# Moving the first transfers of a hybrid encoder layer: sample rows in quarters, norm scales from ScalarE's queue, sinks and later parameters under the first SwiGLU

## The chip, the core and the metric

One core of a Trainium2 chip runs the whole program. The metric is device time in microseconds (us) of one execution; three executions of the kernel before are given. The engines are TensorE (PE), VectorE (DVE), ScalarE (ACT), GpSimd (POOL) and SyncE (SP); each works through its own list of instructions in order. In the kernel before every transfer between DRAM and on-chip memory is asked for from SP's list; the moving itself is done by 16 DMA engines.

## What is computed

One layer of a streaming encoder on 512 prompt rows and 8 x 16 sample rows, all fp32, model width 1024:

```
x += 0.5 * SwiGLU_1(rmsnorm(x) * norm_ffn1)
h  = rmsnorm(x) * norm_mix;  P = h @ w_in
A  = sliding-window attention with per-head sinks (attn_sinks)
B  = HGRN2 linear recurrence;  C = conv(4) -> RG-LRU
x += (sig(gA)*A@w_attn_o + sig(gB)*B@w_hgrn_o + sig(gC)*C@w_lru_o) @ w_out
x += 0.5 * SwiGLU_2(rmsnorm(x) * norm_ffn2)
```

Prompt and sample rows share all weights, so the kernel stacks them into 640 columns. Besides x the kernel needs some small parameter vectors: three norm scales, convolution weights, biases, gate parameters, head norms (together 99 rows of 128 numbers) and the 16 attention sinks.

## The kernel before, in words

The activations are kept transposed, 8 chunks of 128 features by 640 columns. Every fp32 product is made of three products of rounded parts: x is split into a high and a low part (RA for the first SwiGLU's input), and so is each weight tile. A weight tile is 1024 x 128 (512 KB). `proj` asks for it into one of three buffers `wr`, makes the high part `wh` (line 654) and the low part `wl` (line 655), and issues for each of the 8 chunks a set of six matmuls of 320 columns (line 659) into one of two psum buffers `pp`.

At the start `load_x` (line 479) brings x. The prompt comes in four quarters of 256 features (`x0`, 512 KB each), the sample rows in one transfer (`xs`, 512 KB). Each quarter is transposed on TensorE into `me` and `ml`, copied out, scaled by `norm_ffn1` and split by `Norm.split` (lines 599 to 602: high part on ScalarE, low part on VectorE). ScalarE also squares the 20 row tiles (line 505) to get the row sums; `first_rstd` (line 507) turns them into RS, the reciprocal root per column, by ten small products on TensorE (lines 518 and 519). The matmuls of the first SwiGLU do not wait for RS; it multiplies their result (`scaled`, line 662).

`load_params` (line 523) asks for parameter rows one vector at a time into the single buffer `pst`, transposes them on TensorE (line 537) and copies them to PRM. It is called once for `norm_ffn1` inside `load_x`, and once for the 91 later rows (line 695 and 696) before the first SwiGLU. PRM's later rows feed `lru_params` (line 551) and, from the end of the first SwiGLU on, everything else. The sinks go to `SK` by ten transfers in `attention` (lines 744 to 748): for each parity of heads one of 64 partitions x 8 numbers and four of 16 x 8, all read with a stride of two numbers.

The order on each engine is not the order of the text. `Sched.run` (line 236) is a planner: it keeps a model of every engine's time, and again and again takes the operation that can start first by that model; among those that start within 0.04 us it takes the one with the lowest priority number (line 161). An operation made later has a higher number; `lag` lowers it by so many projections (`S.item` counts them). A transfer is 0.47 us on SP by the model, and its data take bytes / 250 GB/s behind the earlier ones (line 287). A buffer of a tag with several slots costs 0.15 us at its first use, a fixed buffer like `SK` nothing, so a transfer into `SK` with no predecessor can be planned at time 0. Because of this, one of the ten sink transfers stands first in SP's list and the others wherever the plan leaves SP free. In the hardware program the engines then wait for each other by semaphores, in that fixed order.

`ffn` (line 677) runs three blocks of 8, 8 and 6 features tiles; in each, two up-projections per tile (gate and value) and then eight down-projections.

Of the kernel before, what the change touches and what calls it, by code (L numbers as in the profile page):

```python
# [16 lines left out]
P = 128  # L17
# [73 lines left out]
def ap_of(x):  # L91
    return x() if isinstance(x, View) else x
# [218 lines left out]
def trunk_kernel(ctx: ExitStack, tc: tile.TileContext, A: dict, O: list):  # L311
    nc = tc.nc
    S = Sched()
# [7 lines left out]
    def dve(n, f, aps=0):  # L321
        return ("DVE", 0.066 + 1.042e-3 * n + 0.063 * aps, f)

    def act(n, f, aps=0, src=None):
        return ("ACT", 0.1 + 0.833e-3 * n + 0.093 * aps - (0.049 if src is not None and src.in_psum else 0.0), f)

    def pol(n, f):
        return ("POOL", 0.1 + n * 1e-3, f)

    def pick(alts, only):  # L330
        return [a for a in alts if only is None or a[0] in only]

    def tt(out, a, b, op, only=None):
        alts = [dve(out.n, lambda: nc.vector.tensor_tensor(out(), a(), b(), op=op))]  # L334
        return S.op(pick(alts, only), [a, b], [out])
# [15 lines left out]
    def fn(out, a, func, scale=1.0, bias=0.0, accum=None):  # L351
        aps = isinstance(scale, View) + isinstance(bias, View) + (accum is not None)
        kw = {}

        def f():
            if accum is not None:
                kw["accum_out"] = accum()
            nc.scalar.activation(out(), a(), func, bias=ap_of(bias), scale=ap_of(scale), **kw)  # L358

        return S.op([act(out.n, f, aps, a)], [a, scale, bias], [out] + ([accum] if accum is not None else []),  # L360
                    func=None if func in ANY_TABLE else func)

    def cp(out, a, only=None):
        alts = [act(out.n, lambda: nc.scalar.copy(out(), a()), 0, a),  # L364
                dve(out.n * (1.0 if a.in_psum else 0.5), lambda: nc.vector.tensor_copy(out(), a()))]
        if only is not None and "POOL" in only:
            alts.append(pol(out.n, lambda: nc.gpsimd.tensor_copy(out(), a())))
        return S.op(pick(alts, only), [a], [out])
# [5 lines left out]
        alts = [pol(out.n, lambda: nc.gpsimd.memset(out(), val)), dve(out.n, lambda: nc.vector.memset(out(), val))]  # L374
        return S.op(pick(alts, only), (), [out])

    def dma(out, a, lag=None):
        v = out if isinstance(out, View) else a
        return S.op([("SP", 0.47, lambda: nc.sync.dma_start(ap_of(out), ap_of(a)))], [a], [out],  # L379
                    dma=v.n * 4 * v.proto.shape[0], lag=lag)  # L380

    def mm(calls):

# [14 lines left out]
    def tr(calls):  # L398

        def f():  # L400
            for o, i, d in calls:
                nc.tensor.transpose(o(), i(), d())  # L402

        return S.op([("PE", sum(0.002 + 0.835e-3 * c[0].n for c in calls), f)], [x for c in calls for x in c[1:]], [c[0] for c in calls])


    def fixed(name, shape, dt=F32):
        return Buf(None, sb(name, shape, dt))

    RA = fixed("RA", [P, 16, T], F32R)  # L410
    RB = fixed("RB", [P, 16, T], F32R)
    RS = fixed("RS", [P, T])
    ident = fixed("ident", [P, P])
# [3 lines left out]
    NPRM = 99  # L417
    PRM = fixed("PRM", [P, NPRM])
# [4 lines left out]
    SK = fixed("SK", [P, 32])  # L423
# [45 lines left out]
    xp = A["x_prompt"][0].rearrange("(t p) d -> p t d", p=P)  # L469
    xs = A["x_sample"].rearrange("b t d -> (b t) d")  # L470
# [5 lines left out]
    def xk(m):  # L476
        return X.v.r("p (k t) -> p k t", k=KD)[:, m, :].at(m)

    def load_x():
        bs = S.buf("xs")  # L480
        xin = []
        for c in range(4):
            b = S.buf("x0")
            v = b.v.r("p (t d) -> p t d", t=4)
            dma(v, xp[:, :, c * 256:(c + 1) * 256], lag=(12, 2.5, 1.9, 1.8)[c])
            xin.append(v)
            if c == 0:
                dma(bs.v, xs, lag=12)
                load_params(("norm_ffn1",), 0, 8, lag=12)
        xv = X.v.r("p (k t) -> p k t", k=KD)  # L490
        for c in range(4):
            pb = S.buf("ml")
            for h in range(2):
                pa, o = S.buf("me"), slice(h * P, (h + 1) * P)
                tr([(pa[:, t * P:(t + 1) * P], xin[c][:, t, o], ident.v) for t in range(4)])
                cp(xk(2 * c + h)[:, 0:TP], pa.v, only=("DVE", "ACT"))
            tr([(pb[:, h * P:(h + 1) * P], bs[:, (2 * c + h) * P:(2 * c + h + 1) * P], ident.v) for h in range(2)])
            for h in range(2):
                cp(xk(2 * c + h)[:, TP:T], pb[:, h * P:(h + 1) * P], only=("DVE", "ACT"))
                n1.split(2 * c + h, xk(2 * c + h))  # L500
        for c in range(4):
            tiles = [xin[c][:, t, :] for t in range(4)] + [bs[:, c * 256:(c + 1) * 256]]
            for t in range(NT):
                j = S.buf("sq")
                fn(j[:, 0:256], tiles[t], AF.Square, accum=ss[:, t, c:c + 1].at((t, c)))
# [14 lines left out]
        cp(RS[:, 0:TP], pa.v, only=one)  # L520
        cp(RS[:, TP:T], pb[:, 0:P], only=one)

    def load_params(names, r0, r1, lag=None):
        b = S.buf("pst")
        for name, r, c in (("norm_ffn1", 0, 8), ("norm_mix", 8, 8), ("norm_ffn2", 16, 8), ("conv_b", 24, 8),
                           ("conv_w", 32, 32), ("lru_b_a", 64, 8), ("lru_b_x", 72, 8), ("lru_lambda", 80, 8),
                           ("hgrn_lb_logits", 88, 8), ("hgrn_o_norm", 96, 1)):
            if name in names:
                src = A[name][0].rearrange("j (k p) -> (j k) p", p=P) if name == "conv_w" else A[name].rearrange("o (k p) -> (o k) p", p=P)
                dma(b[r - r0:r - r0 + c, 0:P].at(r), src, lag=lag)  # L530
        for r, name in ((97, "q_norm"), (98, "k_norm")):
            if name in names:
                for h in range(2):
                    dma(b[r - r0:r - r0 + 1, h * 64:h * 64 + 64].at((r, h)), A[name], lag=lag)
        ps = S.buf("ml")
        n = r1 - r0
        tr([(ps[:, :n], b[:n, :P], ident[:n, :n])])
        cp(PRM[:, r0:r1].at(r0), ps[:, :n], only=("DVE",))

    G1, GM, G2, CVB, CVW, BA, BX, LAM, LBL, ON, QN, KN = 0, 8, 16, 24, 32, 64, 72, 80, 88, 96, 97, 98  # L540

# [45 lines left out]
    def hv(v):  # L587
        return v.r("p (a b) -> p a b", a=2)

    def pv(ps):  # L590
        return ps.v.r("p (a b) -> p a b", a=2)[:, :, :HT]
# [70 lines left out]
    def scaled(tag, ps, late=False):  # L662

        b = S.buf(tag)
        if late:
            cp(hv(b.v), pv(ps), only=("ACT", "DVE"))
            tt(b.v, b.v, RS.v, ALU.mult)
        else:
            tt(hv(b.v), pv(ps), hv(RS.v), ALU.mult)
        return b  # L670

    def parts(R, k, v):
        cp(R[:, k, :].at(k), v, only=("ACT",))
        tt(R[:, 8 + k, :].at(8 + k), v, R[:, k, :].at(k).cast(F32), ALU.subtract)


    def ffn(wu, wd, R, H, sfx, done):
        for f0, nf in ((0, 8), (8, 8), (16, 6)):
            for f in range(nf):
                late = not sfx and f0 + f < 2  # L680
                g = scaled("fA" + sfx, proj(wu, 0, KD, (f0 + f) * P, R), late)
                fn(g.v, g.v, AF.Silu)
                u = scaled("fB" + sfx, proj(wu, 0, KD, FF + (f0 + f) * P, R), late)
                tt(u.v, g.v, u.v, ALU.mult)
                parts(H, f, u.v)
            for m in range(KD):
                ps = proj(wd, f0 * P, nf, m * P, H)
                x = xk(m)
                stt(hv(x), pv(ps), 0.5, hv(x), ALU.mult, ALU.add)
                if f0 == 16:  # L690
                    done(m)
# [1 line left out]
    n1 = Norm(G1, RA)  # L693
    load_x()
    first_rstd()
    load_params(("norm_mix", "norm_ffn2", "conv_b", "conv_w", "lru_b_a", "lru_b_x", "lru_lambda", "hgrn_lb_logits",
                 "hgrn_o_norm", "q_norm", "k_norm"), 8, NPRM)
    nm = Norm(GM, RA)

    def spill(m):  # L700
        nm.add(m)
        dma(XD[m].at(m), xk(m))

    ffn(A["w_ffn1_up"][0], A["w_ffn1_down"][0], RA, RB, "", spill)
    lru_params()
    nm.rstd()
    W = A["w_in"][0]
# [33 lines left out]
    def attention():  # L741
        ck, cv = A["cache_attn_k"][0], A["cache_attn_v"][0]
        sk = A["attn_sinks"][0].rearrange("(m two) -> two m", two=2)
        for h in range(2):
            dma(SK[h * 64:h * 64 + 64, 0:8].at(h), sk[h:h + 1, :].to_broadcast([64, 8]))
            for b in range(4):
                p0 = b * 32 + h * 16
                dma(SK[p0:p0 + 16, 8:16].at((b, h)), sk[h:h + 1, :].to_broadcast([16, 8]))
        ts(SK[:, 16:32], SK[:, 0:16], -1.0, ALU.mult, only=("DVE",))
        ms = S.buf("ms")  # L750
        mi = S.buf("qt")
# [21 lines left out]
        for j in range(2):  # L773
            q, r = qknorm(proj(W, 0, KD, AK + j * P, RA))
            for h in range(2):
                a, b = h * 64, h * 64 + 64
# [4 lines left out]
                ps = S.buf("ml")  # L781
# [7 lines left out]
        for j in range(2):  # L789
            q = scaled("qq", proj(W, 0, KD, AV + j * P, RA))  # L790
            for t0, t1 in ((0, 4), (4, 5)):
                ps = S.buf("me")
# [409 lines left out]
    for m in range(KD):  # L1202
        ps = proj(A["w_out"][0], 0, KD, m * P, RA)
# [52 lines left out]
```

## Time and profile before

| | us |
|---|---|
| median of 3 runs | 1991.15 (1991.13 to 1991.19) |
| the profiled execution | 1991.13 |
| its span, first to last instruction | 1989.3 |
| TensorE busy | 1959.9 (99%) |
| VectorE busy | 1159.4 (58%) |
| ScalarE busy | 557.3 (28%) |
| GpSimd busy | 31.5 (2%) |

Times in the profile count from the span's start. "Busy" leaves out the issuing of transfers, waits and branches. The page says of TensorE that ends of matmuls are modelled, so neighbouring rows can overlap a little. A wait is put down to the event that came last by the profile; when several semaphores are waited for, the name can be that of another one.

### The profile page before, as it was taken

Reading aid. Unit: us, or ns where it says so; the run is one execution under the profiler, and the core shown is the slowest. Engines: PE = TensorE matmul, PEld = TensorE weight load, DVE = VectorE, ACT = ScalarE, POOL = GpSimd, SP = SyncE. Lnnn points to the kernel's source line nnn. Section 1 sums busy time; section 2 is a strip of 40 time slices with the busy share of each in tenths; the row PEclk is TensorE's granted clock in tenths of the full one; section 3 lists DMA queues with packets and bytes.
Section 4 is the critical chain, followed back from the end, with each engine's and each line's share of the span. In section 5 each row is a group of like instructions: output and inputs, shape, how many; then the busy total and the mean of one; then the engine's idle time right before and its main releaser. Section 6 shows DMA issues by size and latency. Waiting matters only on the chain.

```text
span 1989.3 us, 34591 instructions
## 1 busy us (share of the span) xinstructions
PE 1959.9 (99%) x15086; PEld 1915.1 (96%) x15086; DVE 1159.4 (58%) x1922; ACT 557.3 (28%) x978; POOL 31.5 (2%) x61
## 2 busy tenths in 40 slices
PE   6999999999999999999999999999999999999998
PEld 5999999999999999999999999999999999999998
DVE  4543444456677783677557788886555443444444
ACT  5110010012468850798002333334112100110000
POOL 0000000000000000020000000000000000000000
PEclk9999999999999999999999999999999999999999
DMA  4222222224412212222322222223322222222223
GB/s 128 77 75 75 75 75 74 75 67 129 121 54 59 64 49 77 75 58 78 87 77 83 77 77 81 84 77 119 85 75 75 75 75 74 75 75 74 75 64 85
DMA packets 304434, 156.85 MB, mean 79 GB/s; under 512 B 22645, under 2 KB 301782, under 8 KB 304282
## 3 DMA queue, kind: packets, MB, share of 16 engines
q1 hardware_dynamic: 304282, 154.63, 27.0%
q8 instruction: 118, 1.93, 0.4%
q14 instruction: 34, 0.28, 0.0%
HBM read 143.32 MB, written 10.63 MB: 77 GB/s over the span
## 4 chain that ended last, share of the span: by engine, by line
PE 92%; ACT 3%; DVE 2%; SPq 1%; DMA 1%; issue 1%; DVEq 0%; ACTq 0%
PE pp L394 84%; PE me L394 4%; PE ml L394 3%; ACT L358 1%; PE ml L402 1%; ACT AR L358 1%; SPq L379 1%; PE me L402 1%; DVE AR L334 1%; DMA SK<-in_attn_sinks_dram 1%; DVE AR L348 1%; DVE RB L334 0%; DVE AR L996 0%; DMA wr<-in_w_in_dram 0%; DVE wl L655 0%
## 5 line engine op out<-in xcount | busy, mean ns | idle before, releaser
L394 PE MATMUL pp<-RA,wh 128*128 128x320 f32 x5056 | 968.1, 313 | 0.3 <-DVE RA L348 0.3
L394 PEld LDWEIGHTS pp<-RA,wh 128*128 128x128 f32 x5056 | 791.6, 189 | 10.8 <-issue 7.6
L394 PE MATMUL pp<-RA,wl 128*128 128x320 f32 x2528 | 576.7, 309 | 0.0
L394 PE MATMUL pp<-RB,wh 128*128 128x320 f32 x2880 | 539.5, 309 | 0.0
L654 DVE CAST wh<-wr 128x1024 fp32r<-128x1024 f32 (+1 forms) x221 | 151.3, 685 | 600.4 <-PE pp L394 598.8
L394 PEld LDWEIGHTS pp<-RB,wh 128*128 128x128 f32 x2880 | 452.5, 188 | 0.0
L394 PEld LDWEIGHTS pp<-RA,wl 128*128 128x128 f32 x2528 | 423.8, 188 | 0.3 <-DVE wl L655 0.2
L394 PE MATMUL pp<-RB,wl 128*128 128x320 f32 x1440 | 328.3, 309 | 0.0
L655 DVE TENSOR_TENSOR wl<-wr,wh 128x1024 fp32r<-128x1024 f32 (+1 forms) x252 | 302.5, 1200 | 0.6 <-DVE AR L334 0.4
L358 ACT ACTIVATE AR<-AR 128x640 f32<-128x640 f32 (+2 forms) x216 | 147.7, 685 | 522.3 <-DVE AR L334 503.2
L394 PEld LDWEIGHTS pp<-RB,wl 128*128 128x128 f32 x1440 | 241.2, 188 | 0.3 <-DVE wl L655 0.3
L334 DVE TENSOR_TENSOR AR<-AR 128x640 f32<-128x640 f32 (+8 forms) x380 | 198.4, 545 | 38.9 <-ACT AR L358 31.2
L334 DVE TENSOR_TENSOR AR<-pp,RS 128x640 f32<-128x640 f32 x168 | 137.5, 819 | 8.5 <-PE pp L394 8.1
L358 ACT ACT_TABLE_LOAD x97 | 124.5, 1283 | 5.8 <-DVE AR L334 3.7
L364 ACT CAST RA<-AR 128x640 fp32r<-128x640 f32 x30 | 21.8, 728 | 211.9 <-DVE AR L334 205.8
L364 ACT CAST RB<-AR 128x640 fp32r<-128x640 f32 x38 | 27.6, 726 | 177.1 <-DVE AR L334 177.1
L394 PE MATMUL ml<-AR 128*128 128x128 f32 (+6 forms) x576 | 68.3, 314 | 0.0
L394 PEld LDWEIGHTS me<-AR 128*32 128x32 f32 (+2 forms) x2016 | 50.5, 118 | 14.6 <-issue 9.5
L394 PE MATMUL me<-AR 128*32 128x16 f32 (+6 forms) x2016 | 63.9, 206 | 0.0
L364 ACT COPY AR<-me 128x512 f32<-128x512 f32 (+3 forms) x72 | 26.0, 375 | 115.5 <-PE me L402 92.2
L394 PEld LDWEIGHTS ml<-AR 128*128 128x128 f32 (+2 forms) x576 | 46.9, 151 | 11.6 <-ACT AR L364 2.6
L348 DVE SCALAR_TENSOR_TENSOR AR<-AR,PRM 64x512 f32<-64x512 f32 (+6 forms) x92 | 52.0, 582 | 0.9
(111 smaller groups left out, 894.0 us busy)
## 6 DMA issues: line engine op xcount, KB each, us to landing
wr<-in_w_ffn_up_dram SPq DMA_DIRECT2D x88, 512.0 KB
wr<-in_w_in_dram SPq DMA_DIRECT2D x84, 512.0 KB
wr<-in_w_ffn_down_dram SPq DMA_DIRECT2D x32, 512.0 KB
wr<-in_w_ffn_down_dram SPq DMA_DIRECT2D x16, 384.0 KB
wr<-in_w_attn_o_dram SPq DMA_DIRECT2D x8, 512.0 KB
AR<-in_state_hgrn_dram SPq DMA_DIRECT2D x8, 512.0 KB
wr<-in_w_lru_o_dram SPq DMA_DIRECT2D x8, 512.0 KB
out_dram<-AR SPq DMA_DIRECT2D x8, 512.0 KB
```

Source lines behind the costliest of these rows:

```text
L334: alts = [dve(out.n, lambda: nc.vector.tensor_tensor(out(), a(), b(), op=op))]
L348: return S.op([dve(out.n, lambda: nc.vector.scalar_tensor_tensor(out(), a(), ap_of(s), b(), op0=op0, op1=op1), isinstance(s, View))], [a, ...
L358: nc.scalar.activation(out(), a(), func, bias=ap_of(bias), scale=ap_of(scale), **kw)
L364: alts = [act(out.n, lambda: nc.scalar.copy(out(), a()), 0, a), dve(out.n * (1.0 if a.in_psum else 0.5), lambda: nc.vector.tensor_copy(out ...
L379: return S.op([("SP", 0.47, lambda: nc.sync.dma_start(ap_of(out), ap_of(a)))], [a], [out], dma=v.n * 4 * v.proto.shape[0], lag=lag)
L394: nc.tensor.matmul(o(), l(), m(), start=s, stop=e)
L402: nc.tensor.transpose(o(), i(), d())
L654: S.op([act(nk * P, lambda: nc.scalar.copy(h(), r())), dve(nk * P * 0.5, lambda: nc.vector.tensor_copy(h(), r()))], [r], [h], lag=2)
L655: S.op([dve(nk * P, lambda: nc.vector.tensor_tensor(l(), r(), h().bitcast(F32), op=ALU.subtract))], [r, h], [l], lag=1.5)
```

## The change

It does four things. (1) `load_x` asks for the sample rows in four quarters of 128 KB, each right behind the prompt's quarter, with new lags that put quarters 2 to 4 ahead of the second and third weight tile. (2) `norm_ffn1` is asked for from ScalarE's instruction list (`act=True`), first of all. (3) The later parameters are asked for inside the first SwiGLU (before feature tile 4), each transfer with a wait for RS, and transposed before feature tile 8. (4) The ten sink transfers get a wait for PRM, so they come after the later parameters were copied there.

```diff
-    def dma(out, a, lag=None):
+    def dma(out, a, lag=None, after=(), act=False):
         v = out if isinstance(out, View) else a
-        return S.op([("SP", 0.47, lambda: nc.sync.dma_start(ap_of(out), ap_of(a)))], [a], [out],
-                    dma=v.n * 4 * v.proto.shape[0], lag=lag)
+        alts = [("SP", 0.47, lambda: nc.sync.dma_start(ap_of(out), ap_of(a)))]
+        if act:
+            alts = [("ACT", 0.47, lambda: nc.scalar.dma_start(ap_of(out), ap_of(a)))]
+        return S.op(alts, [a, *after], [out], dma=v.n * 4 * v.proto.shape[0], lag=lag)
...
+    def sv(bs, c):
+        return bs[:, c * 256:(c + 1) * 256].at(c)
+
     def load_x():
...
-            dma(v, xp[:, :, c * 256:(c + 1) * 256], lag=(12, 2.5, 1.9, 1.8)[c])
+            lag = (12, 2.7, 2.6, 2.5)[c]
+            if c == 0:
+                load_params(("norm_ffn1",), 0, 8, lag=13, act=True)
+            dma(v, xp[:, :, c * 256:(c + 1) * 256], lag=lag)
+            dma(sv(bs, c), xs[:, c * 256:(c + 1) * 256], lag=lag)
             xin.append(v)
-            if c == 0:
-                dma(bs.v, xs, lag=12)
-                load_params(("norm_ffn1",), 0, 8, lag=12)
...
-    def load_params(names, r0, r1, lag=None):
+    def load_params(names, r0, r1, lag=None, act=False):
         b = S.buf("pst")
+        later = () if act else (RS.v,)
...
-                dma(b[r - r0:r - r0 + c, 0:P].at(r), src, lag=lag)
+                dma(b[r - r0:r - r0 + c, 0:P].at(r), src, lag=lag, after=later, act=act)
...
-    def ffn(wu, wd, R, H, sfx, done):
+    def ffn(wu, wd, R, H, sfx, done, aside=()):
         for f0, nf in ((0, 8), (8, 8), (16, 6)):
             for f in range(nf):
+                for at, job in aside:
+                    if at == f0 + f:
+                        job()
...
-    load_params(("norm_mix", "norm_ffn2", "conv_b", "conv_w", "lru_b_a", "lru_b_x", "lru_lambda", "hgrn_lb_logits",
-                 "hgrn_o_norm", "q_norm", "k_norm"), 8, NPRM)
...
-    ffn(A["w_ffn1_up"][0], A["w_ffn1_down"][0], RA, RB, "", spill)
+    place = []
+
+    def more_params():
+        place.append(load_params(("norm_mix", "norm_ffn2", "conv_b", "conv_w", "lru_b_a", "lru_b_x", "lru_lambda",
+                                  "hgrn_lb_logits", "hgrn_o_norm", "q_norm", "k_norm"), 8, NPRM))
+
+    ffn(A["w_ffn1_up"][0], A["w_ffn1_down"][0], RA, RB, "", spill, ((4, more_params), (8, lambda: place[0]())))
...
-            dma(SK[h * 64:h * 64 + 64, 0:8].at(h), sk[h:h + 1, :].to_broadcast([64, 8]))
+            dma(SK[h * 64:h * 64 + 64, 0:8].at(h), sk[h:h + 1, :].to_broadcast([64, 8]), after=(PRM.v,))
             for b in range(4):
                 p0 = b * 32 + h * 16
-                dma(SK[p0:p0 + 16, 8:16].at((b, h)), sk[h:h + 1, :].to_broadcast([16, 8]))
+                dma(SK[p0:p0 + 16, 8:16].at((b, h)), sk[h:h + 1, :].to_broadcast([16, 8]), after=(PRM.v,))
```

## Rows read from the trace of the kernel before

**Rows 1.** The page, busy time of each engine, its share of the span, and the number of instructions.

```profile
PE 1959.9 (99%) x15086; PEld 1915.1 (96%) x15086; DVE 1159.4 (58%) x1922; ACT 557.3 (28%) x978; POOL 31.5 (2%) x61
```

**Rows 2.** Busy time by stretch. Columns: the stretch and its length; busy us (and instructions) of PE, PEld, DVE, ACT, POOL; the granted TensorE clock as a share of full; the mean busy share of the 16 DMA engines; GB/s.

```profile
0.00:34.40 34.40, 15.99 (x89) 13.73 (x90) 13.88 (x26) 19.38 (x54) 1.66 (x7) 0.97 0.49 139
...
45.00:460.00 415.00, 415.00 (x2834) 415.00 (x2832) 189.85 (x244) 37.04 (x49) 0.56 (x2) 1.00 0.25 74
```

**Rows 3.** What TensorE's matmuls waited for over the whole span: us in total, times, longest.

```profile
PE me L402 <- DMA AR<-in_x_prompt_dram: 11.1, 2, 11.0
PE ml L402 <- DMA SK<-in_attn_sinks_dram: 6.3, 1, 6.3
```

**Rows 4.** Two pieces of the chain of work that ended last, in order of time: start us, us, what.

```profile
19.63 9.68 DMA SK<-in_attn_sinks_dram
...
32.15 2.27 DMA SK<-in_attn_sinks_dram
```

**Rows 5.** SP's timeline: start us, us that the issuing held SP, what is written from where, how many.

```profile
0.74 0.75 SPq L379 DMA_DIRECT2D SK<-in_attn_sinks_dram  x1
1.54 0.60 SPq L379 DMA_DIRECT2D AR<-in_x_prompt_dram  x1
...
2.73 1.74 SPq L379 DMA_DIRECT2D AR<-in_norm_ffn_dram  x1
...
15.28 4.98 SPq L379 DMA_DIRECT2D SK<-in_attn_sinks_dram  x6
...
28.28 0.27 SPq L379 DMA_DIRECT2D AR<-in_lru_lambda_dram  x1
...
31.78 1.27 SPq L379 DMA_DIRECT2D SK<-in_attn_sinks_dram  x3
```

**Rows 6.** DMA packets in three stretches of 1 us: from 3 to 4, from 8 to 9, and from 24 to 25 us. The count "under 512 B" holds the four-byte packets.

```profile
DMA packets 107, 0.00 MB, mean 0 GB/s; under 512 B 107, under 2 KB 107, under 8 KB 107
...
DMA packets 207, 0.27 MB, mean 266 GB/s; under 512 B 54, under 2 KB 171, under 8 KB 207
...
DMA packets 106, 0.00 MB, mean 0 GB/s; under 512 B 106, under 2 KB 106, under 8 KB 106
```

**Rows 7.** Busy time by stretch, columns as in rows 2, around the first data of x.

```profile
5.00:6.00 1.00, 0.00 (x0) 0.00 (x0) 0.00 (x0) 0.00 (x0) 0.00 (x0) 1.00 0.04 0
6.00:7.00 1.00, 0.00 (x0) 0.00 (x0) 0.00 (x0) 0.00 (x0) 0.00 (x0) 1.00 0.24 67
```

**Rows 8.** One weight tile in the steady part of the first SwiGLU: its issue in SP's timeline, then busy time by stretch (columns as in rows 2).

```profile
103.60 0.37 SPq L379 DMA_DIRECT2D wr<-in_w_ffn_up_dram  x1
...
104.50:105.00 0.50, 0.50 (x5) 0.50 (x5) 0.00 (x0) 0.50 (x1) 0.00 (x0) 1.00 0.26 73
105.00:106.00 1.00, 1.00 (x9) 1.00 (x8) 0.82 (x1) 0.07 (x1) 0.00 (x0) 1.00 1.06 316
106.00:107.00 1.00, 1.00 (x9) 1.00 (x8) 0.00 (x0) 0.00 (x0) 0.00 (x0) 1.00 0.58 172
```

**Rows 9.** The end of another weight tile's data by stretch (columns as in rows 2), and the timeline's instruction that waited for a weight tile to land; in brackets its engine's idle time before it and what ended it.

```profile
38.00:39.00 1.00, 1.00 (x6) 1.00 (x5) 0.00 (x1) 0.00 (x0) 0.00 (x0) 0.50 0.58 164
...
39.17 0.69 DVE L654 CAST wh<-wr 128x1024 fp32r<-128x1024 f32 x1 [1.17 <-DMA wr<-in_w_ffn_up_dram]
```

**Rows 10.** Timeline of the first stage, TensorE and VectorE: start us, us, engine, line, operation, number of instructions merged.

```profile
10.96 1.94 PE L402 MATMUL me<-ident,AR 128*128 128x128 f32 x8 [10.96 <-DMA AR<-in_x_prompt_dram]
...
20.33 1.04 PE L402 MATMUL me<-ident,AR 128*128 128x128 f32 x8
...
24.63 1.68 DVE L348 SCALAR_TENSOR_TENSOR RA<-AR,PRM,RA 128x640 fp32r<-128x640 f32 x2 [0.83 <-ACT RA L358]
...
27.60 1.68 DVE L348 SCALAR_TENSOR_TENSOR RA<-AR,PRM,RA 128x640 fp32r<-128x640 f32 x2 [0.83 <-ACT RA L358]
...
34.52 1.42 PE L394 MATMUL pp<-RA,wh 128*128 128x320 f32 x4
...
39.27 0.75 PE L394 MATMUL pp<-RA,wh 128*128 128x320 f32 x4
...
40.15 0.75 PE L394 MATMUL pp<-RA,wh 128*128 128x320 f32 x4
...
44.55 1.28 PE L394 MATMUL me<-ident,SSQ 128*128 128x128 f32 x10
```

**Rows 11.** Busy time by stretch, columns as in rows 2, for the second idle stretch of TensorE and the stretch behind it.

```profile
28.12:34.39 6.27, 0.00 (x0) 0.00 (x1) 1.16 (x2) 1.57 (x7) 0.00 (x0) 0.82 0.34 91
34.39:39.27 4.88, 4.85 (x20) 4.88 (x21) 0.52 (x3) 0.61 (x3) 0.00 (x0) 0.53 0.41 113
```

**Rows 12.** ScalarE between 10 and 31 us by line and operation, the squares of x's row tiles (count, busy us and mean ns, idle before); then two pieces of the timeline: the last square, and the last step of RS's reciprocal root on VectorE.

```profile
L358 ACT ACTIVATE AR<-AR 128x256 f32<-128x256 f32 x18 | 7.5, 418 | 9.1 <-DMA AR<-in_x_prompt_dram 8.8
...
40.06 0.42 ACT L358 ACTIVATE AR<-AR 128x256 f32<-128x256 f32 x1
...
43.34 0.16 DVE L348 SCALAR_TENSOR_TENSOR SSQ<-SSQ 128x5 f32<-128x5 f32 x1
```

**Rows 13.** VectorE's timeline in the steady part of the first SwiGLU: the low part of one weight tile, and the rounding of two later ones, each with VectorE's idle time before it.

```profile
102.35 1.22 DVE L655 TENSOR_TENSOR wl<-wr,wh 128x1024 fp32r<-128x1024 f32 x1
...
122.13 0.69 DVE L654 CAST wh<-wr 128x1024 fp32r<-128x1024 f32 x1 [2.12 <-PE pp L394]
...
129.17 0.69 DVE L654 CAST wh<-wr 128x1024 fp32r<-128x1024 f32 x1 [4.48 <-PE pp L394]
```

More of the change, by code (lines that the diff above doesn't have):

```diff
@@ L496, in load_x @@
                 cp(xk(2 * c + h)[:, 0:TP], pa.v, only=("DVE", "ACT"))
-            tr([(pb[:, h * P:(h + 1) * P], bs[:, (2 * c + h) * P:(2 * c + h + 1) * P], ident.v) for h in range(2)])
+            tr([(pb[:, h * P:(h + 1) * P], sv(bs, c)[:, h * P:(h + 1) * P], ident.v) for h in range(2)])
             for h in range(2):
@@ L501, in load_x @@
         for c in range(4):
-            tiles = [xin[c][:, t, :] for t in range(4)] + [bs[:, c * 256:(c + 1) * 256]]
+            tiles = [xin[c][:, t, :] for t in range(4)] + [sv(bs, c)]
             for t in range(NT):
@@ L533, in load_params, with place @@
                 for h in range(2):
[L534 to L538, printed above, removed]
+                    dma(b[r - r0:r - r0 + 1, h * 64:h * 64 + 64].at((r, h)), A[name], lag=lag, after=later)
+        def place():
+            ps = S.buf("ml")
+            n = r1 - r0
+            tr([(ps[:, :n], b[:n, :P], ident[:n, :n])])
+            cp(PRM[:, r0:r1].at(r0), ps[:, :n], only=("DVE",))
+        if not act:
+            return place
+        place()
     G1, GM, G2, CVB, CVW, BA, BX, LAM, LBL, ON, QN, KN = 0, 8, 16, 24, 32, 64, 72, 80, 88, 96, 97, 98
```

## The prediction

> **What bounds the kernel now.** I read the page first: TensorE is busy 99% of the span, the next engine 58% [rows 1]. So time can only come from TensorE's idle time, from its clock, or from fewer instructions, and this change removes none. The busy time by stretch says where the idle time is: 16.0 us busy in the first 34.4, then 415.0 of 415.0 [rows 2]. Whatever lets TensorE reach the steady part earlier shifts the rest of the kernel by as much, if the steady part stays gapless. The list of waits names two stalls [rows 3]: 11.0 us until the first quarter of x lands, and 6.3 us on a transposition into `ml` (the 91 later parameters), put down to the sinks. The chain of waits runs through sink transfers at the same place [rows 4]. So both stalls point at transfers that nothing needs before attention.
>
> Why are they slow? SP's timeline has a sink transfer first and the first quarter of x behind it at 1.54 [rows 5]. Until 6 us no bytes to speak of move, only 107 small packets a microsecond with 0.04 of the DMA engines busy; x's data begin between 6 and 7 [rows 6, 7]. A weight tile asked for in the steady part has its first data after about 1 us [rows 8]. I read this as the first sink transfer (64 x 8 single numbers, 512 packets, 4.8 us at 107 a microsecond) holding x up. The same pace returns at 24 us, when the next six sinks are under way [rows 6]. The parameters queue behind those: the one for `lru_lambda` leaves SP only at 28.28, three more sinks come at 31.78, and the transposition follows [rows 4, 5].
>
> **The change part by part.**
> *The first quarter of x.* Now TensorE starts on it at 10.96 [rows 10]. After the change it is SP's first transfer, at 0.74 (the sinks' place, rows 5). The steady weight tile, also 512 KB, is issued at 103.60 and moved 0.037 + 0.316 MB until 106; the last 0.17 MB take 0.5 us more, so its last byte is at 106.5, 2.9 after the issue [rows 8]. From a tile's last byte (about 38.5) to the instruction that waited for it (39.17) it is 0.65 [rows 9]. That gives 0.74 + 2.9 + 0.65 = 4.3. The trace shows no large transfer at a cold start; if the 1 us to the first data doubles, 5.2. I take 4.8, between them: **6.2 us earlier** (5.8 to 6.7).
>
> *Norm scales on ScalarE's list.* ScalarE sits idle 9.1 us ahead of its first square [rows 12], so the issue costs it nothing; SP is rid of an issue that held it 1.74 [rows 5]. TensorE's list may begin with their transposition. Even with the 3.5 us of a whole weight tile from issue to landing, 4 KB issued at 0.7 to 2.0 is there at 4.2 to 5.5: between 0 and 0.7 us of delay, and 0 taken, because it is 4 KB.
>
> *Sample rows in quarters; weight tiles 2 and 3 behind all of x.* The bytes are the same, so with 316 GB/s [rows 8] x, sample rows and one weight tile (3.15 MB) are in 10 us after the first data, at 12 to 13, the second weight tile at 14 to 15. Today VectorE splits the last two chunks from 27.60 [rows 10], 21.4 after a shift of 6.2: cover of 8 us. The second tile, split in 2.6 (rounding 0.69, low part 1.22, and 0.7 for what VectorE does between them, rows 13), is ready by 17.5, while TensorE has transpositions and the first projection until about 20. Taken at 0. x's quarters 2 to 4 also land earlier relative to the first; I take no gain for it.
>
> *The parameters' transposition leaves the gap at 28.12.* The gap is 6.27 us [rows 11]. In its place stand matmuls whose inputs exist: eight of the sixteen sets of the first two projections are done by then (two per finished chunk), chunks 4 and 5 are split at 24.63 + 1.68 = 26.3, so four sets of 0.88 us (40.15 - 39.27, rows 10) last to 31.6, and chunks 6 and 7 are split at 27.60 + 1.68 = 29.3. No new wait there. The transposition itself is done later (0.2 us). **6.1 us.**
>
> *The clock behind the gap.* During and after the idle 6.27 us the granted clock falls: 0.53 of full from 34.39 to 39.27, the 1.2 GHz level [rows 11]. Three sets took 39.27 - 34.52 = 4.75 us there, against 3 x 0.88 = 2.64 [rows 10]. Without the gap: **2.1 us.**
>
> *What is late next.* RS needs all 20 squares, then the ten small products that now start at 44.55 [rows 10]. ScalarE works almost without a pause from x's landing at 10.9 until 28.12 + 1.57 = 29.7 [rows 11], 18.8 us, with 18 of the squares [rows 12]; two more (0.42 each with a read of the sum behind it, 0.55 by estimate) and one copy out of `pp` (0.7, as the rounding in rows 13) make 20.6. From the end of the last square to the end of the last step on VectorE it is 43.50 - 40.6 = 2.9 [rows 12]. With x at 4.8, the small products can start at 4.7 + 20.6 + 2.9 = 28.2. TensorE by the sum below reaches that place at 44.55 - 14.4 = 30.15. So ScalarE has 1.9 us of cover; and TensorE cannot gain more than 44.55 - 28.2 = 16.3 (16.8 with x at 4.3). That is the upper bound of the gain.
>
> *New waits on SP.* The 13 later parameter transfers wait for RS; weight loads planned behind them wait too. In the steady part a tile is asked for at 103.60 and is the one rounded at 122.13, three roundings later; TensorE needs it only when the next rounding starts, at 129.17 [rows 8, 13]. With 2.6 for the split it must have landed by 126.5, 22.9 after the issue, and it needs 3.5. So a load can be 19.4 us late without a stall. RS is some microseconds off its planned time at most: 0.
>
> *The sinks in mid SwiGLU.* They follow PRM's copy, after 24 projections of eight sets (7.0 us each), around 185 us. 2 x 512 + 8 x 128 = 2048 packets take 19.3 us at 106 a microsecond [rows 6]. A weight load right behind all of them lands 19.3 + 3.5 = 22.8 after its issue, against 22.9: just hidden. While bulk data moved, from 8 to 9 us, there were at most 54 small packets [rows 6]; in the steady part bulk moves for 0.25 of the time [rows 2], so 0.75 x 106 + 0.25 x 54 = 93 a microsecond, 22 us, 2.6 of them open. From 0 to 2.6; I take 0.3, as a load rarely falls right behind the sinks, and balance it against x's later quarters. No operation of the first SwiGLU but `lru_params` reads the later parameters; its small steps move under the matmuls, where VectorE is under half busy [rows 2]: 0.
>
> **Sum**: 6.2 + 6.1 + 2.1 = 14.4, off the profiled execution's 1991.13 (span 1989.3 and 1.8 around it; the median is 1991.15): **1976.7 us**.
>
> **The rivals.**
> *A. The first transfer is slow by itself.* x's 4.6 us from issue to data could be a cold start rather than the sinks. For it: nothing large is moved earlier in the trace. Against: small packets flow in those microseconds, and the next sinks delay what follows them in the same way at 20 to 28 us. Then x gains only 1.54 - 0.74 = 0.8 and the sum is 9.0: 1982.1. Chance 0.10.
>
> *B. TensorE stays at its low clock longer.* Eight transpositions took 1.94 us at the start and 1.04 at 20.33 [rows 10], so the first stage runs at 1.2 GHz for a while, although the stretches list 1.00. With quarters that arrive spread out and the second projection's tile behind them, TensorE's early work is thinner. If sixteen more transpositions (2 x 0.9) and four sets (0.7 each) fall at the low level, 4.6 us are lost: 1981.3. Against: most of this would pass under ScalarE's 20.6 us. Chance 0.07. The Trainium skill (TensorE: Matmul & The Clock Gate, Part 1) says that the default state is the throttled one and activity releases it; the two durations agree, and by that rule a thin start is paid at half rate.
>
> *C. The sinks stall the weights: slower.* If four-byte packets and weight tiles share the queue at 54 a microsecond throughout, 2048 take 38 us and a load behind them is 38 + 3.5 - 22.9 = 18.5 late; with the clock's 2.1, 1976.7 + 20.6 = 1997. It decides against the change below 65 packets a microsecond: 2048 / 65 = 31.5, a stall of 12.1, and 2.1 more make 14.2. For it: the 54. Against: that figure includes the end of the sinks, and the steady part leaves the DMA engines idle three quarters of the time. Chance 0.05.
>
> *D. The gap moves instead of closing.* The order is planned with modelled times, and by it the ten small products or the second projection could stand where their inputs are late, the idle time of 6.1 and the clock's 2.1 coming back: 1985 if all of it. Against: the cover of 1.9 and about 3 us worked out above. Chance 0.06; a remainder of 0.02 is no change at all, for a reason that I do not see.
>
> **How the numbers follow.** Forecast 0.70, with 1974.0 (the upper bound of the gain, 16.8, is 1974.3) to 1979.5 (x at 5.2, 2.6 at the sinks). A and B lie at 1981 to 1982.1, so the range to **1982.5** holds about 0.85 and leaves out C and most of D. About 0.2%, 4 us, is what a measurement can tell from no change: faster 0.92, same 0.03, slower 0.05.
>
> **What would show it.** Right: TensorE's first transposition of x at 4.3 to 5.2; no idle stretch above 2 us from then to 460 us; granted clock 1.00 without a break; the ten small products at 28 to 31; ten sinks in SP's timeline past 150 us, weight tiles behind them late but TensorE's busy time full. Wrong: x's data still beginning past 5 us (A); matmul sets at twice their time after 15 us (B); idle time on `wr` around 185 to 215 us (C); a wait of several microseconds ahead of the small products (D).

## The result and the profile after

The changed kernel takes **1980.61 us** (median of 5 runs, 1979.81 to 1984.12) against 1991.19 of the kernel before in the same series: a ratio of 0.9949, 95% interval 0.9938 to 0.9960. That is 10.6 us faster; 14.4 were forecast. The time lies in the range on record (1974.0 to 1982.5), 1.1 us above the part of it that the likeliest case was given (to 1979.5).

The profiled execution took 1981.24 us, with a span of 1979.5. Busy time by stretch, with the columns of [rows 2]:

```profile
0.00:34.40 34.40, 27.97 (x174) 27.21 (x175) 21.63 (x40) 24.65 (x64) 1.66 (x7) 1.00 0.60 170
34.40:195.00 160.60, 160.60 (x1097) 160.59 (x1096) 73.86 (x103) 16.12 (x22) 0.00 (x0) 1.00 0.27 76
195.00:206.00 11.00, 11.00 (x77) 11.00 (x76) 1.20 (x10) 0.75 (x1) 0.00 (x0) 1.00 0.20 49
206.00:208.00 2.00, 0.75 (x6) 0.49 (x4) 1.12 (x5) 0.74 (x2) 0.00 (x0) 1.00 0.00 0
208.00:210.00 2.00, 1.03 (x4) 0.94 (x4) 2.00 (x4) 0.00 (x0) 0.00 (x0) 0.78 0.22 66
210.00:212.00 2.00, 2.00 (x9) 1.90 (x8) 1.21 (x3) 1.16 (x2) 0.00 (x0) 0.50 0.24 68
212.00:214.00 2.00, 2.00 (x14) 2.00 (x13) 2.00 (x4) 1.07 (x2) 0.00 (x0) 0.87 0.69 200
214.00:460.00 246.00, 246.00 (x1679) 246.00 (x1678) 113.48 (x139) 21.79 (x30) 0.57 (x2) 1.00 0.27 77
```

TensorE works 28.0 us of the first 34.4, where it was 16.0 in [rows 2]. The steady part is full on both sides of one place: at 206 to 210 TensorE is idle for some 2.2 us, VectorE was nearly idle for the 11 us ahead of it, and the granted clock falls to 0.50 (the 1.2 GHz level) before it is back at 214. The lists of waits name both ends of it: four lines of TensorE over the whole span, and one of VectorE between 45 and 460 us (us in total, times, longest).

```profile
PE me L404 <- DMA AR<-in_x_prompt_dram: 4.0, 2, 2.0
PE ml L404 <- DMA AR<-in_norm_ffn_dram: 2.3, 1, 2.3
PE pp L396 <- DVE AR L334: 2.2, 1, 2.2
PE me L396 <- DVE NL L334: 2.0, 3, 0.9
...
DVE SK L340 <- DMA SK<-in_attn_sinks_dram: 8.8, 1, 8.8
```

Of the two waits of [rows 3], the one on the later parameters is gone, and the one for x is down from 11.1 us to 4.0. New are 2.2 us of TensorE behind VectorE, and 8.8 us of VectorE behind the sinks. The timeline shows how the second makes the first. These are rows of TensorE, VectorE and SP, in order of time: start us, us, then as in [rows 5, 10].

```profile
0.74 0.44 SPq L379 DMA_DIRECT2D AR<-in_x_prompt_dram  x1
...
4.53 1.97 PE L404 MATMUL me<-ident,AR 128*128 128x128 f32 x8 [2.00 <-DMA AR<-in_x_prompt_dram]
...
8.90 1.94 PE L404 MATMUL me<-ident,AR 128*128 128x128 f32 x8 [1.98 <-DMA AR<-in_x_prompt_dram]
...
12.67 1.27 PE L396 MATMUL pp<-RA,wh 128*128 128x320 f32 x4
...
22.33 0.75 PE L396 MATMUL pp<-RA,wh 128*128 128x320 f32 x4
...
24.97 0.75 PE L396 MATMUL pp<-RA,wh 128*128 128x320 f32 x4
...
25.05 0.48 SPq L379 DMA_DIRECT2D AR<-in_norm_mix_dram  x1
...
28.49 1.28 PE L396 MATMUL me<-ident,SSQ 128*128 128x128 f32 x10
...
29.58 0.89 DVE L365 COPY RS<-me 128x512 f32<-128x512 f32 x2 [1.35 <-PE me L396]
...
58.55 0.69 DVE L667 CAST wh<-wr 128x1024 fp32r<-128x1024 f32 x1 [4.48 <-PE pp L396]
...
181.22 2.18 SPq L379 DMA_DIRECT2D SK<-in_attn_sinks_dram  x3
...
186.61 0.25 DVE L365 COPY PRM<-ml 128x91 f32<-128x91 f32 x1
...
192.42 0.69 DVE L667 CAST wh<-wr 128x1024 fp32r<-128x1024 f32 x1 [0.50 <-PE pp L396]
...
194.89 0.17 DVE L340 TENSOR_SCALAR AR<-AR 128x8 f32<-128x8 f32 x1
203.88 0.17 DVE L340 TENSOR_SCALAR SK<-SK 128x16 f32<-128x16 f32 x1 [8.83 <-DMA SK<-in_attn_sinks_dram]
...
207.50 0.69 DVE L667 CAST wh<-wr 128x1024 fp32r<-128x1024 f32 x1
208.10 0.82 DVE L334 TENSOR_TENSOR AR<-pp,RS 128x640 f32<-128x640 f32 x1
208.97 1.34 PE L396 MATMUL pp<-RA,wh 128*128 128x320 f32 x4 [2.22 <-DVE AR L334]
...
486.52 0.41 DVE L365 COPY HIST<-ml 128x256 f32<-128x256 f32 x1
```

Read it from the end of the stall. TensorE's matmuls at 208.97 need a psum buffer that VectorE empties at 208.10. VectorE empties it behind the rounding of the next weight tile at 207.50. The rounding before that ran at 192.42, and one comes every 7.04 us, so this one was due at 199.46: it is 8.0 us late. Ahead of it in VectorE's list stands one small instruction at 203.88, the negation of the sinks (`ts(SK[:, 16:32], ...)` in `attention`), which was reached at 195.05 and waited 8.83 us for the sinks to land. Behind it 3.6 us of small steps of `lru_params` remain, with their own wait of 1.6 us for ScalarE ahead of 206.78. Attention, where the negated sinks are first used, comes long after (543.9). My reading of the planner, which no run tests by itself: its model prices a transfer by its bytes (at 250 GB/s), so sinks of 2 KB and less count as there about 2 us after their issue, and the negation can stand here.

To measure shifts I take two instructions of the same kind in every kernel: the eighth rounding of a weight tile, after which the first SwiGLU runs evenly, and the copy to HIST, behind the first SwiGLU. In the kernel before (VectorE's timeline; the row at 37.83 is the same negation of the sinks there):

```profile
37.83 0.17 DVE L340 TENSOR_SCALAR SK<-SK 128x16 f32<-128x16 f32 x1 [2.73 <-DMA SK<-in_attn_sinks_dram]
...
72.85 0.69 DVE L654 CAST wh<-wr 128x1024 fp32r<-128x1024 f32 x1 [4.48 <-PE pp L394]
...
496.59 0.42 DVE L365 COPY HIST<-ml 128x256 f32<-128x256 f32 x1
```

So the start gains 72.85 - 58.55 = **14.3 us**, and by HIST 496.59 - 486.52 = 10.1 are left: **4.2 us are given back** between them. At 206 to 214 the stretches give 2.2 us of idle time and, at the lower clock, about 2 x (0.22 + 0.50 + 0.13) = 1.7. From HIST to the end it is 1492.7 us before and 1493.0 after.

### The profile page after: what moved, and what is told of

It is laid out like the page before. It is cut to its first block, busy times and chain, and to the rows that moved or that the text cites. A ratio compares the mean times of both kernels' runs of the same rounds, so it can differ in the third digit from the quotient of the medians.

```text
span 1979.5 us, 34587 instructions
## 1 busy us (share of the span) xinstructions
PE 1960.8 (99%) x15086; PEld 1917.2 (97%) x15086; DVE 1159.5 (59%) x1921; ACT 560.6 (28%) x981; POOL 31.5 (2%) x61
## 4 chain that ended last, share of the span: by engine, by line
PE 93%; DVE 3%; ACT 3%; DMA 1%; issue 1%; SPq 0%; DVEq 0%; ACTq 0%
PE pp L396 84%; PE me L396 4%; PE ml L396 3%; ACT L358 1%; PE ml L404 1%; ACT AR L358 1%; PE me L404 1%; DVE AR L334 1%; DVE AR L348 1%; DMA SK<-in_attn_sinks_dram 1%; DMA AR<-in_x_prompt_dram 0%; SPq L379 0%; DVE wl L668 0%; DVE RB L334 0%; DVE AR L1016 0%
## 5 line engine op out<-in xcount | busy, mean ns | idle before, releaser
L358 ACT ACT_TABLE_LOAD x99 | 127.0, 1283 | 13.9 <-DVE AR L334 11.1
```

## The experiments

Two theories for each half. Of the start: **S**, the sinks' single four-byte packets ahead of x and of the parameters were what held both up; against it **A**, the first large transfer is slow by itself, and **P**, the later parameters cost time in the gap wherever the sinks are. Of the loss: **V**, VectorE's in-order wait at the negation; against it **W**, weight tiles that land late behind the sinks. The later runs ask which property of the sinks matters, and what the other three parts of the change are worth.

**e1: the negation planned later.** In the changed kernel, one edit:

```diff
-        ts(SK[:, 16:32], SK[:, 0:16], -1.0, ALU.mult, only=("DVE",))
+        ts(SK[:, 16:32], SK[:, 0:16], -1.0, ALU.mult, only=("DVE",), after=(RS.v,))
```

`after` is an additional input for the planner (`ts` hands it on to `S.op`), here RS as the second norm writes it.

> The changed kernel, with the negation of the sinks on VectorE planned only after the second norm (some 300 us later); the transfers stay where they are. Theory V (the shortfall is VectorE's in-order wait of 8.8 us on the sinks in the first SwiGLU, which holds up a weight tile's rounding and a psum copy): no idle time of TensorE and no drop of its clock from 195 to 215 us, time 1980.6 - 4.2 = 1976.4. Rival W (the weight tile that queues behind the sinks is itself late, the prediction's C): idle time on the weight tile remains, 1980 or more.

Measured: 1977.64 us (1976.84 to 1978.16), ratio 0.9930 (0.9916 to 0.9943), span 1975.4. VectorE's timeline:

```profile
58.61 0.69 DVE L667 CAST wh<-wr 128x1024 fp32r<-128x1024 f32 x1 [4.48 <-PE pp L396]
...
199.52 0.69 DVE L667 CAST wh<-wr 128x1024 fp32r<-128x1024 f32 x1 [0.73 <-PE pp L396]
...
482.46 0.41 DVE L365 COPY HIST<-ml 128x256 f32<-128x256 f32 x1
```

The start is that of the changed kernel. The rounding that came at 207.50 comes at 199.52, and HIST 4.06 us earlier. The sinks are asked for at the same place (181.28) and the weight tiles stand behind them as before, so V holds and W falls. The median is 1.2 us above the 1976.4 expected: between the profiled executions the whole 4.06 shows (1981.24 to 1977.18), between the medians 3.0.

**e2: the sinks back at the start.** e1 without `after=(PRM.v,)` on the ten sink transfers, so that one of them is again SP's first.

```diff
-            dma(SK[h * 64:h * 64 + 64, 0:8].at(h), sk[h:h + 1, :].to_broadcast([64, 8]), after=(PRM.v,))
+            dma(SK[h * 64:h * 64 + 64, 0:8].at(h), sk[h:h + 1, :].to_broadcast([64, 8]))
...
-                dma(SK[p0:p0 + 16, 8:16].at((b, h)), sk[h:h + 1, :].to_broadcast([16, 8]), after=(PRM.v,))
+                dma(SK[p0:p0 + 16, 8:16].at((b, h)), sk[h:h + 1, :].to_broadcast([16, 8]))
```

> As the run before, with the sinks' wait for the parameters taken away, so that one sink transfer of 512 numbers is SP's first again and the nine others follow the first weight tiles. Theory S (sinks at the head hold x up): TensorE's first transposition of x at 10.5 to 11.3 instead of 4.5, time 1976.4 + 6.2 = 1982.6. Rival A (the first large transfer is slow by itself at a cold start, and x gained only because it moved 0.8 us up): x by 5.5, time 1977.2.

Measured: 1982.02 us (1981.72 to 1982.58), ratio 0.9953 (0.9939 to 0.9966). The timeline of SP, TensorE and VectorE:

```profile
0.73 0.73 SPq L379 DMA_DIRECT2D SK<-in_attn_sinks_dram  x1
1.52 0.60 SPq L379 DMA_DIRECT2D AR<-in_x_prompt_dram  x1
...
10.77 1.97 PE L404 MATMUL me<-ident,AR 128*128 128x128 f32 x8 [8.29 <-DMA AR<-in_x_prompt_dram]
...
14.52 1.94 PE L404 MATMUL me<-ident,AR 128*128 128x128 f32 x8 [1.35 <-DMA AR<-in_x_prompt_dram]
...
63.39 0.69 DVE L667 CAST wh<-wr 128x1024 fp32r<-128x1024 f32 x1 [4.48 <-PE pp L396]
```

x is back at 10.8, where it was in [rows 10]: S holds, A falls. The other reading is as useful. x comes 6.4 us earlier in e1 (at 4.42) than in e2, but the eighth rounding only 63.39 - 58.61 = **4.8**. The other 1.6 go at the second quarter of x. In e1 its transposition waits 3.42 us, in e2 1.35:

```profile
10.24 1.94 PE L404 MATMUL me<-ident,AR 128*128 128x128 f32 x8 [3.42 <-DVE RA L348]
```

That is 2.1 us lost, of which the first two matmul sets behind it win back 0.5. The wait is put down to VectorE, but ScalarE's next square of x waits for the transfer too, until 10.19, so the quarter itself was not there.

**e3: the later parameters back before the SwiGLU.** e1 with the parameters asked for and transposed where the kernel before does it, and the sinks asked for before feature tile 8 (`load_sinks` holds the ten transfers, each with `after=(RB[:, 7, :].at(7),)`, the last tile of the first block).

```diff
-        later = () if act else (RS.v,)
+        later = ()
...
-    ffn(..., spill, ((4, more_params), (8, lambda: place[0]())))
+    load_params(("norm_mix", ..., "k_norm"), 8, NPRM)()
+    ffn(..., spill, ((8, load_sinks),))
```

> As the first run, with the later parameters asked for and transposed ahead of the first SwiGLU as in the kernel before, and the sinks asked for in the SwiGLU's second block as now. Theory S (the second stall came from the sinks ahead of the parameters): TensorE waits less than 1 us for the parameters, time 1976.4 to 1977.4. Rival P (the parameters' own place ahead of the SwiGLU is what stalls): 4 to 6 us of idle time and the low clock behind it return, 1982 to 1985.

Measured: 1977.64 us (1977.08 to 1977.98), ratio 0.9930 (0.9916 to 0.9944); the eighth rounding at 59.74. The parameters' transposition stands at 24.28 with no idle time ahead of it. P falls: the parameters cost a stall only with sinks ahead of them. The eighth rounding is 1.1 us later than in e1; the medians of the two do not show it, and this one is 0.2 above the range expected.

**e4: the kernel before with the sinks alone moved.** None of the other three parts.

```diff
-            dma(SK[h * 64:h * 64 + 64, 0:8].at(h), sk[h:h + 1, :].to_broadcast([64, 8]))
+            dma(SK[h * 64:h * 64 + 64, 0:8].at(h), sk[h:h + 1, :].to_broadcast([64, 8]), after=(RB[:, 7, :].at(7),))
...
-                dma(SK[p0:p0 + 16, 8:16].at((b, h)), sk[h:h + 1, :].to_broadcast([16, 8]))
+                dma(SK[p0:p0 + 16, 8:16].at((b, h)), sk[h:h + 1, :].to_broadcast([16, 8]), after=(RB[:, 7, :].at(7),))
-        ts(SK[:, 16:32], SK[:, 0:16], -1.0, ALU.mult, only=("DVE",))
+        ts(SK[:, 16:32], SK[:, 0:16], -1.0, ALU.mult, only=("DVE",), after=(RS.v,))
```

> The kernel before with the sinks alone moved (asked for in the first SwiGLU's third block, negated after the second norm); sample rows in one transfer, norm scales on SP, parameters early. Theory S: both stalls go, 1991.2 - 14.3 = 1976.9, up to 1978.5 if the sample rows in one piece cost something. Rival A: 1991.2 - 9.0 = 1982.2. Rival P: the first stall goes and the second stays, 1985.

Measured: **1976.15 us** (1975.94 to 1976.83), ratio 0.9923 (0.9910 to 0.9937), span 1974.5. The timeline of SP, TensorE and VectorE:

```profile
4.39 1.94 PE L402 MATMUL me<-ident,AR 128*128 128x128 f32 x8 [4.39 <-DMA AR<-in_x_prompt_dram]
...
22.04 0.24 PE L402 MATMUL ml<-ident,AR 91*128 91x91 f32 x1
...
58.38 0.69 DVE L654 CAST wh<-wr 128x1024 fp32r<-128x1024 f32 x1 [4.48 <-PE pp L394]
...
300.74 11.22 SPq L379 DMA_DIRECT2D SK<-in_attn_sinks_dram  x10
...
318.86 0.69 DVE L654 CAST wh<-wr 128x1024 fp32r<-128x1024 f32 x1 [4.48 <-PE pp L394]
...
326.51 0.69 DVE L654 CAST wh<-wr 128x1024 fp32r<-128x1024 f32 x1 [5.10 <-DMA wr<-in_w_ffn_down_dram]
...
482.12 0.41 DVE L365 COPY HIST<-ml 128x256 f32<-128x256 f32 x1
```

The whole gain of the start is here: 72.85 - 58.38 = 14.5. x starts at 4.39, and the parameters' transposition at 22.04 waits for nothing. The time is 0.75 us below the range expected (1976.9 to 1978.5). The ten sinks at 300.74 do make one weight tile late. Of VectorE's 5.1 us ahead of 326.51 most is its usual wait for TensorE (4.48 ahead of 318.86); at 7.04 us a tile this rounding was due at 325.90, so it is 0.6 us late. TensorE is busy for all of the stretch around it, so that is covered (busy time by stretch, columns as in [rows 2]):

```profile
34.40:460.00 425.60, 425.60 (x2904) 425.60 (x2903) 195.83 (x247) 40.10 (x54) 0.57 (x2) 1.00 0.27 76
```

No other kernel here is faster by more than the runs can tell.

**e5: the sinks at the start, read contiguously.** e2 with one edit, which fills SK with other sinks than the heads need:

```diff
-        sk = A["attn_sinks"][0].rearrange("(m two) -> two m", two=2)
+        sk = A["attn_sinks"][0].rearrange("(two m) -> two m", two=2)
```

> e2 with one edit: the sinks are read in two contiguous halves instead of the even and the odd ones (so SK holds other sinks than the heads need), and each partition's eight numbers lie side by side in DRAM. The queue's order and the number of transfers stay. Theory S (it is the single four-byte packets, 512 for the first transfer at 106 to 107 a microsecond, that hold x up): the first transfer is 64 pieces of 32 bytes, 0.6 us at the same pace, x is first transposed at 10.8 - 4.2 = about 6.6, and the median falls by 4 us from e2's 1982.0 to about 1978. Rival Q (any small transfer ahead of x on the queue costs the 5 to 6 us, whatever its pieces): x at 10.8 again and 1982.

**e9: a smaller transfer of single numbers first.** e2 with the loop over the four 16 x 8 transfers put ahead of the 64 x 8 one; SP's first is then one of 16 x 8.

> e2 with the 64 x 8 and the 16 x 8 sink transfers asked for in the other order, so that the transfer ahead of x has 128 single numbers in place of 512; the engines' other lists stay. Theory S (a transfer of single numbers ahead of x costs its own issue, 0.6 us, and its packets at 107 a microsecond): x first transposed at 4.4 + 0.6 + 128 / 107 = 6.2, against 10.8 with 512 packets (worked out the same way 9.8) and 5.1 in e5; median about 1977.5 to 1978.5. Rival Q2 (a fixed delay whenever single numbers lie ahead): x near 10 again, 1981 to 1982.

Measured: e5 1977.51 us (1977.08 to 1978.33), ratio 0.9930 (0.9915 to 0.9945); e9 1977.85 us (1977.58 to 1978.08), ratio 0.9931 (0.9913 to 0.9948). The timeline of SP and TensorE, of e5 and then of e9:

```profile
1.36 0.57 SPq L379 DMA_DIRECT2D AR<-in_x_prompt_dram  x1
...
5.13 1.97 PE L404 MATMUL me<-ident,AR 128*128 128x128 f32 x8 [2.65 <-DMA AR<-in_x_prompt_dram]
```

```profile
1.19 0.42 SPq L379 DMA_DIRECT2D AR<-in_x_prompt_dram  x1
...
5.83 1.97 PE L404 MATMUL me<-ident,AR 128*128 128x128 f32 x8 [3.22 <-DMA AR<-in_x_prompt_dram]
```

From the issue of x's first quarter to TensorE's first transposition of it:

| ahead of x on SP | us |
|---|---|
| nothing (the changed kernel, 0.74 to 4.53) | 3.8 |
| 64 pieces of 32 bytes (e5) | 3.8 |
| 128 pieces of 4 bytes (e9) | 4.6 |
| 512 pieces of 4 bytes (e2) | 9.2 |

The transfer's place costs only its own issue on SP; the rest is its separate pieces, 5.4 us for 512 and 0.8 for 128, against 4.8 and 1.2 at the pace of [rows 6]. Both came earlier than expected (e5 at 5.13 for 6.6, e9 at 5.83 for 6.2). Both rivals, a price for any small transfer and a fixed delay, fall.

**e10: the changed kernel with the sinks read contiguously.** The edit of e5, made in the changed kernel itself; the order on every engine stays that of the change, the early negation included.

> The changed kernel with one edit: the sinks read in two contiguous halves (so SK holds other sinks), each partition's eight numbers side by side in DRAM. The order on every engine stays, VectorE's negation of the sinks included, whose place is reached at 195 us. Theory V+S (the negation waits because 2048 single packets from 181 us take until 203.9): 256 pieces of 32 bytes take 2.4 us at the same pace, the last of them is asked for at 192.9 and lands by about 195 to 196, the negation waits under 1 us, TensorE keeps no idle time at 207 and the median is that of e1, 1977.6 within 0.7. Rival L (the sinks are late because they are asked for late and wait behind weight tiles on the queue, whatever their pieces): the negation still waits 5 us or more, 1980 to 1981.

Measured: 1977.45 us (1976.64 to 1977.77), ratio 0.9928 (0.9912 to 0.9944). VectorE's timeline:

```profile
194.48 0.17 DVE L340 TENSOR_SCALAR SK<-SK 128x16 f32<-128x16 f32 x1
...
481.91 0.41 DVE L365 COPY HIST<-ml 128x256 f32<-128x256 f32 x1
```

The negation stands where it did and waits for nothing. So the stall takes both halves: a reader planned early, and pieces that need some 20 us. Removing either one gives the same time within what the runs can tell (e1 1977.64, e10 1977.45).

**e6, e7, e8: the other three parts, one at a time on e4.** e6 adds the moved parameters, e7 `norm_ffn1` from ScalarE's list, e8 the quarters with their lags, each as in the change's diff.

> e4 (the kernel before with the sinks alone moved) with part 3 of the change added: the later parameters asked for in the first SwiGLU and transposed before feature tile 8. In e4 their transposition stands on TensorE at 22.0 us without a wait. If parts 1 to 3 cost or bring nothing beside the sinks: 1976.15 within 0.5. If the parameters' 13 issues on SP between 9.7 and 18.7 us still cost something (weight tile 2 asked for later): 0.3 to 1 us less than e4, 1975.2 to 1975.9. If lru_params' small steps or the later wait on VectorE cost: above 1976.7.

> e4 with part 2 of the change added: norm_ffn1 from ScalarE's list. If it is hidden, as I took it: x first transposed at 4.4 as in e4, and 1976.15 within 0.5. If SP's freed 1.7 us bring x's later quarters forward and these count: down to 1975.

> e4 with part 1 of the change added: the sample rows in quarters and the new lags. e1 has all four parts without the sinks' stall and is 1.5 us slower than e4, so some part costs 1.5 us. If it is this one (the second quarter of the prompt waits behind nothing, but the second weight tile waits behind all of x): 1977.2 to 1977.8, with TensorE's second transposition or a weight tile's wait showing it in the first 20 us. If it is not: 1976.15 within 0.5.

| | median us | x first transposed | HIST |
|---|---|---|---|
| e4 | 1976.15 (1975.94 to 1976.83) | 4.39 | 482.12 |
| e6, parameters | 1976.51 (1976.17 to 1977.06) | 4.47 | 481.90 |
| e7, norm scales | 1976.29 (1975.75 to 1976.51) | 4.57 | 481.62 |
| e8, quarters | 1976.92 (1976.32 to 1977.57) | 4.49 | 482.31 |

The three parts move HIST by -0.2, -0.5 and +0.2 us; by the medians they are 0.4, 0.1 and 0.8 slower than e4, with ranges that overlap; the kernel before was 0.3 slower beside these three (1991.62) than beside e4 (1991.31). None of them is worth anything that these runs can tell once the sinks are out of the way. e8's 1976.92 lies between the two cases that were written down for it (up to 1976.65, or 1977.2 to 1977.8) and decides for neither. The 1.5 us between e1 and e4 that I set out to place are not placed on one part: 0.3 lie before HIST (482.46 against 482.12), 0.5 behind it (1492.9 us to the end against 1492.4), and the rest is not in the profiled executions.

## Why the prediction was right, and where it was not

**The whole: inside the range, partly by luck.** The forecast was 14.4 us and 10.6 came. The range reached beyond 1979.5 only to hold A and B, and neither brought the time there; what did is a wait that no rival describes. The start came out as forecast, and one term after it failed.

**The sum at the start: right, and nearly so in its terms.** Cut TensorE's way at three places that both kernels have: the first transposition of x, the ninth matmul set, and the twelfth, which starts 33.58 us before the eighth rounding in both. In the kernel before they start at 10.96, 34.52 and 39.27, with the eighth set's end at 28.12 [rows 10, 11]; in the changed kernel at 4.53, 22.33 and 24.97.

| | measured | forecast |
|---|---|---|
| x earlier (10.96 - 4.53) | 6.4 | 6.2 |
| the gap and the clock behind it (39.27 - 28.12, less three sets, 2.64) | 8.5 | 6.1 + 2.1 = 8.2 |
| from x to the ninth set (17.16 before, 17.80 after) | -0.6 | 0 |
| sum, the eighth rounding | 14.3 | 14.4 |

x lies at 4.53, inside 4.3 to 5.2. The small loss between x and the ninth set stands where the forecast took 0. It is not the later quarters: the second group of transpositions follows the first by 4.37 us here and by 4.58 before. The second matmul set is slow (1.27 us at 12.67 for its first four matmuls, 0.75 in the kernel before), and a little also the third group (1.18 and 1.04). The terms are not independent: beside e2, where all else is as in e1, an x that comes 6.4 us earlier is worth 4.8.

**Which edit closes the gap.** The forecast gave the gap's end to moving the parameters' transposition. The parameters need not move: with the sinks gone they are transposed at 22.0 and 24.3 without a wait (e4, e3). Moving them does close it with the sinks still early (e2). Either suffices, so the edits' gains don't add. The rows had said it: the parameters queued behind six sinks [rows 5].

**What was right.** Norm scales: transposed at 2.29, ahead of x, at no cost; e7 agrees. Quarters and the weight tiles behind all of x: 0 taken, 0.2 us lost by HIST in e8. What is late next: the bound for the ten small products, worked out as 28.2, was met at 28.49, earlier than the 30.15 at which the sum had TensorE there, because in the new list 15 instead of 17 sets stand ahead of them; nothing waited for them, so D did not come. A fell by e2, e4 and e5, as argued from the packets. That slow set is B, in small. By their durations the second group of eight transpositions runs at the low level in both kernels (1.94 us at 8.90 here, 1.97 before), though the stretches list 1.00; the third no longer quite (1.18 at 14.27, 1.04 before). The second matmul set does so only here. With the third group that is some 0.9 us, against the 4.6 of B. TensorE could hardly have used it: in this order the small products can't start before the last step of RS's root ends, at 28.23, 0.3 us ahead of where they do. The Trainium skill (TensorE: Matmul & The Clock Gate, Part 1) has the throttled half-rate state as the default. The trace agrees with 1.97 us for eight transpositions at 4.53, against 1.04 later.

**New waits on SP: the right cost for a wrong reason.** The 13 parameter transfers were said to wait for RS, and the sinks for PRM. They wait for neither. The first parameter leaves SP at 25.05, RS is written from 29.58 on; the first sinks leave at 181.22, PRM is copied at 186.61. `after` only shapes the plan, and the hardware program keeps no wait for it in these rows.

**The step that failed: "The sinks in mid SwiGLU", 0 to 2.6 us with 0.3 taken and balanced away.** It measured 4.2, and e1 brings 4.1 of it back. The transfer itself was sized well: 19.3 to 22 us for 2048 packets, and from the first issue at 181.22 to the negation at 203.88 it is 22.7. What was wrong is who waits for it. I looked only at weight tiles behind the sinks on SP's queue, where the 19.4 us of slack held (VectorE waits for no weight tile here; in e4 one is 0.6 us late and TensorE does not feel it), and at `lru_params`, whose reader I took as hidden because VectorE is under half busy. I did not ask which instruction reads SK, and where it stands in VectorE's list. The kernel before has the same instruction waiting 2.73 us at 37.83, and I did not carry that over. C is wrong in the same way: it priced the sinks against weight tiles, and its 65 packets a microsecond were not the question. Between 195 and 200, while VectorE waits, 562 small packets move, 112 a microsecond:

```profile
DMA packets 562, 0.00 MB, mean 0 GB/s; under 512 B 562, under 2 KB 562, under 8 KB 562
```

Two of the signs listed, "no idle stretch above 2 us" and "granted clock 1.00 without a break", failed at this one place and led to it.

## What to carry to other kernels

A transfer that is moved moves its readers' wait with it: before pricing the queue, find the first instruction that reads its data and what stands behind that instruction on its in-order engine, however small it is. Where several edits aim at one stall, test each by itself: here one of four gave everything (1976.15 us alone with its reader planned late, 1980.61 for all four with the reader early), and their forecast gains did not add. Count pieces, not bytes: 2048 four-byte pieces took over 20 us. The Trainium skill (DMA: Bandwidth & Descriptors, Rules for kernel authors) says that a strided last dimension becomes one descriptor per element, and advises to make it contiguous. The trace agrees: x is transposed 5.6 us earlier in e5 than in e2, and HIST copied 4.6 us earlier in e10 than in the changed kernel (0.5 of it from ahead of the negation's place).

## What the runs showed of the hardware that was not expected

A transfer of 2 KB in 512 separate numbers holds back a 512 KB transfer asked for next on the same queue by 5.4 us, and as many numbers in 64 pieces of 32 bytes by nothing that shows (3.8 us from issue to use in both). VectorE's standstill of 8.8 us with TensorE at work cost TensorE 2.2 us of idle time, and almost as much again by the clock: a pause of 2.2 us behind a stretch that was full at a granted clock of 1.00 was followed by 0.50, the 1.2 GHz level, from 210 to 212 us, and by 1.00 again from 214.
